# The down projection of a decoder step as Strassen's seven products over the whole sum, with its operands combined on GpSimd during the up projection

## The chip, the cores and the metric

One core of a Trainium2 chip runs the whole step in one launch. The metric is the device time of one execution in microseconds (us). The engines: TensorE (PE; PEld is its weight load), VectorE (DVE), ScalarE (ACT), GpSimd (POOL, "Pool" below) and SyncE (SP), which issues most DMAs.

## The reference

One inference step of a hybrid decoder layer: 1024 prompt tokens and 8 x 8 sample tokens, 1088 rows of 1024 channels. After the mixing sub-layer comes the channel sub-layer, which the change is about:

```python
    h2 = x * (1 + sc2) + sh2
    val, gt = jnp.split(h2 @ w_up, 2, axis=-1)
    gt_c, ffn_state = _causal_dwconv(gt, ffn_prev, w_fdw, b_fdw)
    f = (jax.nn.gelu(gt_c, approximate=False) * val) @ w_down
    x = _layernorm(ALPHA * x + (1 + g2) * f, ln2_g, ln2_b)
```

Here `w_up` is 1024 x 5632, `w_down` 2816 x 1024, the convolution 3 wide, and all values are float32.

## The kernel before, in words

Matmul operands are held in two parts: `split` (L551 to L553) writes a rounded high part on ScalarE (L552, type fp32r) and the residue on VectorE (L553). A product takes three passes for the prompt rows (high x high, high x low, low x high), and two for the sample rows, whose two parts share one stationary tile.

**Up projection.** A column block f (of NFF = 22, 128 channels of the value and 128 of the gate) is one step. It already runs by Strassen's seven products (in Winograd's form) over its block: `up_weights(f)` loads the gate's and the value's weights (L1724, L1725, into the ring `raw` of three buffers), Pool makes four combinations of 512 columns (L1728, L1729, L1730, L1733), and seven splits write the weight tiles W[0] to W[6], each held once, so that W[i] of the next block is written after product i of this block. `up` (matmuls at L1752) walks through the seven products; `evacuate` adds partial results into the tiles `vt` (value) and `gp` (gate) with the operations at L1675 to L1687, each reading PSUM. `gate` applies the width-3 convolution on VectorE (L1769 to L1773, into `gc`), gelu on ScalarE (L1774) and the product with the value on Pool (L1776, 128 x 1088); then SyncE stores the block to the DRAM scratch `fscr` (L1777) and its sample columns to `fsscr` (L1778). Blocks run in the order f = 0, 1, ..., 21.

**Down projection.** The 22 blocks are summed in three groups, GROUPS = (0..7), (8..14), (15..21). In each group all nine row tiles (eight of the prompt, `tt` = 8 for the sample) are multiplied by the group's weights:

```python
    for grp, (f0, f1) in enumerate(GROUPS):
        for tt in range(9) if grp < 2 else (8, *range(8)):
...
            fx, passes = f_tile(grp, tt)
...
            for i in range(nf):
...
                for xt, wt in passes:
                    for c in cs_:
                        PE.matmul(pd[c], fx[:, xt, i], w[:, wt, cw * c:cw * c + cw],
...
```

`f_tile` loads a row tile's operands from `fscr` (L1860) and splits them into `ft`; `prefetch` loads and splits whole weight rows of 1024 columns into `wd`, a ring of NW = 12. Group 0 copies its sums into `acc` (L1898), group 1 adds (L1900) and puts in the gated sum and the residual (Pool at L1904 and L1905, VectorE at L1906 and L1907), and group 2 ends each row tile with `finish`: gate, sum, statistics (L1824 to L1827), the norm (L1836 to L1846) and the store of `y`.

The order of instructions on each engine is set by the framework's scheduler before the run; at run time each engine takes its instructions strictly in that order.

## Time and profile before

| | |
|---|---|
| median of three runs | 1494.72 us (1490.79 to 1496.66) |
| the profiled execution: its own time | 1499.9 us |
| the profiled execution: its span | 1498.1 us, 27014 instructions |
| busy: PE / DVE / ACT / POOL | 1425.9 / 1102.5 / 611.2 / 579.4 us |
| up projection | about 775 to 1221 us of the span |
| down projection | 1226 to 1498 us |
| HBM read / written | 184.31 / 32.68 MB |

The span is what the profile covers; the execution's own time lies 1.8 us over it. Times in the rows further down are counted from the span's start. A duration of VectorE or ScalarE overlaps with the next instruction's by some 0.08 us, so that the step from start to start is a little shorter than the busy time.

### The profile page before, as it was taken

To read this page: it belongs to the slowest core of one execution; us is meant where nothing else is said; L and a number is where in the kernel's file an instruction comes from. 1 tells how busy PE (TensorE), PEld (TensorE's weight loads), DVE (VectorE), ACT (ScalarE), POOL (GpSimd) and SP (SyncE) were. 2 spreads that over 40 slices of the span, in tenths; PEclk is the share of its full clock that TensorE was granted. 3 is DMA by queue.
4 is the path that set the end of the run, shared out by engine and by line. 5 is a ranking of instruction groups with operands and counts; after the bars stand their busy time and mean duration, and the time that the engine had idled before them with its cause. 6 is when DMAs were issued, how large, how long until landed. Compare 5 with 4: busy or idle time off the path is not lost.

```text
span 1498.1 us, 27014 instructions
## 1 busy us (share of the span) xinstructions
PE 1425.9 (95%) x10302; PEld 1237.2 (83%) x10302; DVE 1102.5 (74%) x1935; ACT 611.2 (41%) x1212; POOL 579.4 (39%) x425
## 2 busy tenths in 40 slices
PE   7999889988999999899989999999999989999997
PEld 4898789985656566578779999999999988888886
DVE  5799999447576756767778777778777764268798
ACT  2534414627787868614353333333333333031110
POOL 0497722116353543524344444344433422016300
PEclk9999999989999999999989999999999999999999
DMA  9755432155868777453213222222222257142331
GB/s 340 244 173 173 149 118 96 73 218 184 289 253 294 270 256 282 159 163 119 77 62 101 73 87 72 82 67 85 75 84 73 73 151 263 47 161 87 112 99 70
DMA packets 116987, 219.26 MB, mean 146 GB/s; under 512 B 28673, under 2 KB 71210, under 8 KB 116602
## 3 DMA queue, kind: packets, MB, share of 16 engines
q1 hardware_dynamic: 113498, 206.03, 41.5%
q0 software_dynamic: 3360, 11.51, 2.1%
q8 instruction: 81, 1.33, 0.3%
q14 instruction: 48, 0.39, 0.1%
HBM read 184.31 MB, written 32.68 MB: 145 GB/s over the span
## 4 chain that ended last, share of the span: by engine, by line
PE 65%; DVE 4%; DMA 2%; ACT 2%; issue 1%; POOL 1%; SPq 0%; DVEq 0%; POOLq 0%; ACTq 0%
PE pu L1752 22%; PE pd L1883 18%; PE scr L1752 7%; PE pu L1451 3%; PE z L1062 2%; PE scr L1451 2%; PE acc L1072 2%; PE acc L1261 2%; PE scr L1205 2%; DMA kv<-kv 1%; PE z L1017 1%; PE z L1022 1%; PE scr L1244 1%; ACT l L820 1%; DVE lh L1055 1%
## 5 line engine op out<-in xcount | busy, mean ns | idle before, releaser
L1883 PE MATMUL pd<-wd,ft 128*128 128x512 f32 (+1 forms) x1186 | 263.0, 385 | 4.4 <-ACT ft L552 4.4
L1883 PEld LDWEIGHTS pd<-wd,ft 128*128 128x128 f32 x1186 | 218.7, 190 | 48.7 <-ACT ft L552 5.0
L1752 PE MATMUL pu<-X,wA 128*128 128x272 f32 x768 | 187.6, 288 | 0.0
L1752 PE MATMUL pu<-Y,wA 128*128 128x272 f32 x756 | 186.7, 288 | 0.0
L1058 POOL TENSOR_TENSOR ll<-l,lh 127x512 fp32r<-127x512 f32 (+4 forms) x92 | 98.2, 1070 | 154.2 <-DVE lh L1055 108.9
L589 PE MATMUL po<-HH,whi 128*128 128x378 f32 (+1 forms) x464 | 152.7, 338 | 0.0
L589 PE MATMUL po<-HL,whi 128*128 128x378 f32 (+1 forms) x464 | 151.8, 333 | 0.5 <-DVE HL L553 0.4
L589 PE MATMUL po<-HH,wlo 128*128 128x378 f32 (+1 forms) x464 | 151.6, 333 | 0.0
L820 ACT ACTIVATE l<-z 127x512 f32<-127x512 f32 (+14 forms) x272 | 121.0, 478 | 52.7 <-PE z L1022 19.6
L1752 PEld LDWEIGHTS pu<-X,wA 128*128 128x128 f32 x768 | 141.5, 188 | 0.0
L1752 PEld LDWEIGHTS pu<-Y,wA 128*128 128x128 f32 x756 | 140.7, 189 | 0.0
L677 DVE SCALAR_TENSOR_TENSOR pc<-u,vec,pc 128x1024 f32<-128x1024 f32 x80 | 102.6, 1282 | 1.3
L1728 POOL TENSOR_TENSOR cc__8820<-raw 128x512 f32<-128x512 f32 x20 | 36.6, 1830 | 168.6 <-DMA raw<-w_up 151.4
L589 PEld LDWEIGHTS po<-HH,whi 128*128 128x128 f32 x464 | 87.1, 190 | 7.9 <-ACT whi L552 3.3
L589 PEld LDWEIGHTS po<-HH,wlo 128*128 128x128 f32 x464 | 87.6, 190 | 4.3 <-issue 3.7
L553 DVE TENSOR_TENSOR wA<-raw,wA 128x512 fp32r<-128x512 f32 x60 | 75.8, 1263 | 20.2 <-ACT wA L552 20.1
L589 PEld LDWEIGHTS po<-HL,whi 128*128 128x128 f32 x464 | 86.9, 188 | 3.9 <-issue 1.7
L661 POOL TENSOR_TENSOR cv<-cv,q 128x1024 f32<-128x1024 f32 x36 | 88.7, 2464 | 3.1 <-ACT q L660 1.4
L552 ACT ACTIVATE wA<-raw 128x512 fp32r<-128x512 f32 x60 | 38.0, 633 | 121.8 <-PE pu L1752 65.6
L1027 DVE SCALAR_TENSOR_TENSOR l<-l,z 127x512 f32<-127x512 f32 (+4 forms) x96 | 53.2, 556 | 38.8 <-ACT l L820 37.9
L1055 DVE CAST lh<-l 127x512 fp32r<-127x512 f32 (+4 forms) x96 | 51.7, 542 | 35.9 <-ACT l L820 24.0
L552 ACT ACTIVATE ft<-fr 128x896 fp32r<-128x896 f32 (+3 forms) x27 | 25.5, 943 | 126.4 <-PE pd L1883 121.5
(654 smaller groups left out, 3633.0 us busy)
## 6 DMA issues: line engine op xcount, KB each, us to landing
kv<-kv SPq DMA_DIRECT2D x128, 512.0 KB
catt<-w_ada SPq DMA_DIRECT2D x48, 512.0 KB
...
```

What stands on the lines that cost most here:

```text
L552: A.activation(hi, x, AF.Copy)
L553: V.tensor_sub(lo, x, hi)
L589: PE.matmul(ps[c][:, 0:b - a], wt[:, 128 * kt:128 * kt + 128], xt[:, kt, a:b], start=first and kt == 0, stop=last and kt == KT - 1)
L661: G.tensor_tensor(op, op, t[:, 0:TP], op=OP.add)
L677: V.scalar_tensor_tensor(pcs[c], src, w, pcs[c], op0=OP.mult, op1=OP.add)
L820: A.activation(out, in_, f, **kw)
L1027: V.scalar_tensor_tensor(out, e, ZMAX, z, op0=OP.min, op1=OP.max)
L1055: V.tensor_copy(t.hl[0], t.l)
L1058: (V if eng == "DVE" else G).tensor_tensor(t.hl[1], t.l, t.hl[0], op=OP.subtract)
L1451: PE.matmul(po[c](), xs()[:, xt, kt % 4], WO[kt][:, wt, 512 * c:512 * c + 512], start=kt == KORD[0] and (xt, wt) == passes[0], stop=kt == ...
L1752: PE.matmul(p[g][:, 0:NB], W[i][wt][:, 128 * kt:128 * kt + 128], X[g][kt][xt][:, i, :], start=i < 3 and kt == 0 and n == 0, stop=kt == 3 a ...
L1883: PE.matmul(pd[c], fx[:, xt, i], w[:, wt, cw * c:cw * c + cw], start=i == 0 and (xt, wt) == passes[0], stop=i == nf - 1 and (xt, wt) == pa ...
```

## The change

The order of blocks in the up projection becomes f = 0, 11, 1, 12, ..., 10, 21, so that after every second block the tiles f = j and f = j + 11 are both on the chip. `combine` lets Pool make four combinations of them (128 x 512 each) and SyncE stores these to a DRAM scratch `sscr`. `down_weights` loads a half of the down projection's weight rows j and j + 11, lets Pool make four combinations (128 x 256 each) in the one buffer `tw`, and SyncE stores them to the scratch `tscr`. For a block f < 11 only the first half of its prompt columns is stored to `fscr`. The buffer `gc` of the gate is held once instead of twice.

The down projection then takes the whole sum of 22 blocks as a 2 x 2 problem: rows 0..511 and 512..1023, blocks 0..10 and 11..21, columns 0..511 and 512..1023, with seven products s of 11 tiles each (s = 0 to 5 and 7), operand by operand of the weights; s = 6 holds weights that only the sample rows need, which are multiplied without combining. Weights are loaded in halves of 512 columns (88 loads for 22), the ring `wd` holds NW = 18 of them, and row tiles of 11 x 128 columns are loaded per product. `half` does gate, residual and statistics of a row tile's half as soon as its sum is complete, `finish` the norm.

```diff
-NW = 12
+NW = 18
-GROUPS = ((0, 8), (8, 15), (15, NFF))
+NH = NFF // 2
+FO = [f for j in range(NH) for f in (j, j + NH)]
...
+    sscr = drp.tile([128, 4, NH, 512], F32, "sscr")
+    tscr = drp.tile([NH, 2, 128, D], F32, "tscr")
...
-        c = dp.tile([128, 4, NB], F32, "gc", bufs=2)
+        c = dp.tile([128, 4, NB], F32, "gc", bufs=1)
...
-        SY.dma_start(fscr[:, :, f, :], v4[:, :, 0:256])
+        n = 2 if f < NH else 4
+        SY.dma_start(fscr[:, 0:n, f, :], v4[:, 0:n, 0:256])
...
+    def combine(j, va, vb):
+        (a11, a21), (a12, a22) = ([v[:, h, :, 0:256] for h in range(2)] for v in (va, vb))
+        so = [dp.tile([128, 2, 256], F32, "so", bufs=2) for _ in range(2)]
+        def one(o, x, y, op, k):
+            G.tensor_tensor(o, x, y, op=op)
+            SY.dma_start(sscr[:, k, j, :].rearrange("p (g i) -> p g i", g=2), o)
+        one(so[0], a21, a22, OP.add, 0)
+        one(a21, a11, a21, OP.subtract, 2)
+        one(so[1], so[0], a11, OP.subtract, 1)
+        one(dp.tile([128, 2, 256], F32, "so", bufs=2), a12, so[1], OP.subtract, 3)
...
+    def down_weights(j, c):
+        t = dp.tile([128, 2, 2, 256], F32, "tw", bufs=1)
+        part = lambda a: a.rearrange("p (b x) -> p b x", b=2)[:, :, 256 * c:256 * c + 256]
+        for i in range(2):
+            SY.dma_start(t[:, i], part(d["w_down"][j + NH * i]))
+        b11, b12, b21, b22 = (t[:, i, b] for i in range(2) for b in range(2))
+        G.tensor_tensor(b11, b12, b11, op=OP.subtract)
+        G.tensor_tensor(b12, b22, b12, op=OP.subtract)
+        G.tensor_tensor(b22, b22, b11, op=OP.subtract)
+        G.tensor_tensor(b21, b22, b21, op=OP.subtract)
+        for i in range(2):
+            SY.dma_start(part(tscr[j, i]), t[:, i])
...
-    for f in range(1, NFF):
-        if f > 1:
+    for n in range(1, NFF):
+        f = FO[n]
+        if n > 1:
             up_weights(f)
...
         gelu = gate(f, *t)
+        if n % 2:
+            combine(n // 2, before, v)
+        down_weights((n - 1) // 2, (n - 1) % 2)
+        before = v
+    down_weights(NH - 1, 1)
...
+    def half(tt, c, parts=1):
...
+        x = ep.tile([128, 512], F32, "fx", bufs=2)
+        SY.dma_start(x[0:n], xscr[t0:t0 + n, H[c]])
+        G.tensor_tensor(x[0:n], x[0:n], rows[0][0:n, 0, H[c]], op=OP.mult)
+        G.tensor_tensor(x[0:n], x[0:n], rows[0][0:n, 1, H[c]], op=OP.add)
...
+        def rest(i):
...
+            V.tensor_mul(a[0:n, p], a[0:n, p], g2["p" if tt < 8 else "s"][0:n, H[c]][:, p])
+            V.tensor_add(a[0:n, p], a[0:n, p], x[0:n, p])
+            V.bn_stats(fst[tt][0:n, parts * c + i, :], a[0:n, p])
...
+    SRC_W = [(lambda j, i=i, c=c: d["w_down"][j + NH * i][:, H[c]]) if k == "b" else (lambda j, i=i, c=c: tscr[j, i][:, H[c]])
+             for k, i, c in (("b", 0, 0), ("b", 1, 0), ("t", 1, 0), ("t", 1, 1), ("t", 0, 1), ("t", 0, 0), ("b", 0, 1), ("b", 1, 1))]
+    SRC_A = [plain(0, 0), plain(0, 1), plain(2, 1), mixed_(1), mixed_(2), mixed_(0), None, mixed_(3)]
...
+    def product(p, lhs, s, passes, cs, start=True, stop=True):
+        for j in range(NH):
+            w = ws[NH * s + j]
+            for x, k in passes:
+                PE.matmul(p, lhs(x, j), w[:, k, cs], start=start and j == 0 and (x, k) == passes[0],
+                          stop=stop and j == NH - 1 and (x, k) == passes[-1])
...
+    for s in range(8):
+        if s > 5:
+            prefetch(NH * (s + 1))
+            sample(s)
...
+        for q in range(4):
+            lhs = a_tile(s, q)
+            prefetch(NH * (s + 1))
...
+            product(p, lhs, s, FULL, ALL)
+            if s == 0:
+                A.activation(c22, p, AF.Copy)
+            elif s == 1:
+                V.tensor_add(c11, c22, p)
...
+            elif s == 5:
+                V.tensor_add(c22, c22, p)
+                V.tensor_add(c12, c12, p)
+                half(q + 4, 1)(0)
+                finish(q + 4)
+            else:
+                V.tensor_add(c12, c12, p)
+                half(q, 1)(0)
+                finish(q)
+            prefetch(min(len(ws) + 3, NH * s + NW))
```

What the scheduler makes of it on Pool, in the middle of the up projection. Before, one block's five operations, in this order (`cc__8820` is the buffer of one combination, `raw` the loaded weights, `vt` and `gc` value and gate):

```order
L1728 TENSOR_TENSOR cc__8820<-raw 128x512
L1729 TENSOR_TENSOR raw<-raw 128x512
L1730 TENSOR_TENSOR raw<-cc__8820,raw 128x512
L1776 TENSOR_TENSOR vt<-vt,gc 128x1088
L1733 TENSOR_TENSOR raw<-raw 128x512
```

After, a stretch of the first half of the blocks: the last of one block's sums, the gelu product (now L1780), and up to the next block's first sum (now L1732):

```order
L1733 TENSOR_TENSOR raw<-raw 128x512
L1807 TENSOR_TENSOR tw<-tw 128x256
L1734 TENSOR_TENSOR raw<-cc__8822,raw 128x512
L1780 TENSOR_TENSOR vt<-vt,gc 128x1088
L1808 TENSOR_TENSOR tw<-tw 128x256
L1793 TENSOR_TENSOR so<-vt 128x512
L1809 TENSOR_TENSOR tw<-tw 128x256
L1793 TENSOR_TENSOR vt<-vt 128x2x256
L1793 TENSOR_TENSOR so<-so,vt 128x512
L1810 TENSOR_TENSOR tw<-tw 128x256
L1737 TENSOR_TENSOR raw<-raw 128x512
L1793 TENSOR_TENSOR so<-vt,so 128x512
```

The four sums of one `tw` group (L1807 to L1810) stand between the sums that feed the next block's weights. Behind these rows come L1807, L1808, L1809, L1732 and L1810 of the next group, then L1733, L1734 and L1780; in the following block two groups stand in one piece each. Groups go on so, two to a block, through the first ten blocks of the loop and end there; in the second half a pair of blocks holds its ten operations of before and the four combinations of L1793.

SyncE in the same stretch, after (before, it held `raw`, `raw`, `fscr` and `fsscr` per block and nothing else):

```order
L1812 DMA tscr<-tw 256x1x256
L1794 DMA sscr<-so 128x512
L1794 DMA sscr<-vt 128x2x256
L1794 DMA sscr<-so 128x512
L1812 DMA tscr<-tw 256x1x256
L1805 DMA tw<-w_down 128x2x256
L1794 DMA sscr<-so 128x512
L1805 DMA tw<-w_down 128x2x256
L1729 DMA raw<-w_up 128x1024
L1812 DMA tscr<-tw 256x1x256
L1728 DMA raw<-w_up 128x1024
L1812 DMA tscr<-tw 256x1x256
```

A weight load for the next block (L1728, L1729) stands behind the stores and loads of `tw`, each of which waits for Pool or for the store before it.

VectorE in the down projection, product s = 5, one row tile (`pd` is PSUM, `fr` and `raw` are the loaded operands, now split at L557):

```order
L1991 TENSOR_TENSOR acc_14318<-acc_14318,pd 128x512
L1992 TENSOR_TENSOR acc_14314<-acc_14314,pd 128x512
L1886 SCALAR_TENSOR_TENSOR fw<-fw 128x1
L557 TENSOR_TENSOR ft<-fr,ft 128x1408
L1870 TENSOR_TENSOR acc_14318<-acc_14318,g2p 128x512
L557 TENSOR_TENSOR wd<-raw,wd 128x512
L1887 TENSOR_SCALAR fw<-fw 128x1
L1871 TENSOR_TENSOR acc_14318<-acc_14318,fx 128x512
L1888 TENSOR_TENSOR fw<-fw 128x1
L1872 BN_STATS fs_14327<-acc_14318 128x6
L1890 SCALAR_TENSOR_TENSOR fy<-fy,fw,rows_14806 128x512 x2
L1881 BN_AGGR fw<-fs_14327 128x2
```

The splits for the coming products (L557) stand in one queue with the sums, the gate and the norm of the row tiles that are finished.

## Rows read from the trace of the kernel before

**Rows 1.** the page's first part: busy time, share of the span, instructions.

```profile
PE 1425.9 (95%) x10302; PEld 1237.2 (83%) x10302; DVE 1102.5 (74%) x1935; ACT 611.2 (41%) x1212; POOL 579.4 (39%) x425
```

**Rows 2.** stretches: length, busy us of PE, PEld, DVE, ACT, POOL, clock, DMA share, GB/s.

```profile
1000.00:1100.00 100.00, 100.00 (x801) 100.00 (x800) 77.05 (x148) 31.66 (x67) 39.91 (x24) 1.00 0.26 80
...
1300.00:1350.00 50.00, 50.00 (x223) 41.40 (x222) 27.79 (x27) 12.35 (x13) 5.86 (x2) 1.00 0.41 131
...
1400.00:1450.00 50.00, 50.00 (x223) 41.40 (x222) 44.88 (x67) 8.52 (x16) 5.04 (x2) 1.00 0.35 108
```

**Rows 3.** single lines and the tile raw: duration ns min/median/max, first and last start us.

```profile
L1733 POOL TENSOR_TENSOR raw<-raw x20: 1285/1291/1630, 796.6 to 1192.8; 128x512 f32<-128x512 f32 x20
...
L1776 POOL TENSOR_TENSOR vt<-vt,gc x22: 2527/2535/4138, 791.8 to 1228.8; 128x1088 f32<-128x1088 f32 x22
...
L553 DVE TENSOR_TENSOR wd<-raw,wd x22: 1211/1224/2960, 1223.4 to 1407.6; 128x1024 fp32r<-128x1024 f32 x22
```

**Rows 4.** Pool in time: start us, us, engine, line, operation, idle before.

```profile
950.16 1.31 POOL L1728 TENSOR_TENSOR cc__8820<-raw 128x512 f32<-128x512 f32 x1 [8.42 <-DMA raw<-w_up]
951.54 2.16 POOL L1729 TENSOR_TENSOR raw<-raw 128x512 f32<-128x512 f32 x1
954.53 1.30 POOL L1730 TENSOR_TENSOR raw<-cc__8820,raw 128x512 f32<-128x512 f32 x1 [0.83 <-DVE wA L553]
955.80 2.54 POOL L1776 TENSOR_TENSOR vt<-vt,gc 128x1088 f32<-128x1088 f32 x1
```

**Rows 5.** VectorE in time, the same columns.

```profile
950.24 2.31 DVE L1772 SCALAR_TENSOR_TENSOR gc<-gp,vec,gc 128x1024 f32<-128x1024 f32 x1
...
954.31 0.41 DVE L1677 TENSOR_TENSOR gp<-vt,pu 128x256 f32<-128x256 f32 x1
...
956.54 2.35 DVE L553 TENSOR_TENSOR wA<-raw,wA 128x512 fp32r<-128x512 f32 x1 [0.66 <-ACT wA L552]
...
966.89 0.68 DVE L553 TENSOR_TENSOR cb__8914<-raw,cb__8914 128x512 fp32r<-128x512 f32 x1
967.49 0.17 DVE L1760 COPY fop<-gp 128x2 f32<-128x2 f32 x1
967.56 0.81 DVE L1769 TENSOR_SCALAR gc<-gp,vec 128x1024 f32<-128x1024 f32 x1
...
968.58 1.28 DVE L1772 SCALAR_TENSOR_TENSOR gc<-gp,vec,gc 128x1024 f32<-128x1024 f32 x1
969.78 0.28 DVE L1773 SCALAR_TENSOR_TENSOR gc<-gs,vec,gc 128x64 f32<-128x64 f32 x1
...
1422.44 1.22 DVE L1831 TENSOR_TENSOR acc<-acc,fx 64x1024 f32<-64x1024 f32 x1 [4.49 <-DMA fx<-acc]
```

**Rows 6.** SyncE in time, the same columns.

```profile
946.57 0.33 SPq L1725 DMA_DIRECT2D raw<-w_up  x1
...
1417.98 0.51 SPq L1830 DMA_DIRECT2D fx<-acc  x1
```

**Rows 7.** waits, 800 to 1200 us: who waited, total us, times, longest.

```profile
POOL cc__8820 L1728 <- DMA raw<-w_up: 140.2, 17, 8.6
```

**Rows 8.** operations by form, 1225 to 1500 us: busy us, mean ns, idle before.

```profile
L1883 PE MATMUL pd<-wd,ft 128*128 128x512 f32 x1102 | 253.0, 392 | 4.4 <-ACT ft L552 4.4
...
L1846 DVE SCALAR_TENSOR_TENSOR fy<-fy,fw,rows 128x512 f32<-128x512 f32 x16 | 11.3, 748 | 0.2
...
L1839 DVE SCALAR_TENSOR_TENSOR fy<-acc,fw,rows 128x1024 f32<-128x1024 f32 x8 | 10.3, 1283 | 0.2
L1883 PE MATMUL pd<-wd,ft 128*128 128x256 f32 x84 | 10.2, 283 | 0.0
```

**Rows 9.** stretches at the start of the down projection, columns as in rows 2.

```profile
1226.00:1235.00 9.00, 9.00 (x27) 6.76 (x28) 8.49 (x7) 6.41 (x6) 4.14 (x1) 0.67 0.93 284
```

**Rows 10.** TensorE in time, columns as in rows 4.

```profile
1225.94 6.30 PE L1883 MATMUL pd<-wd,ft 128*128 128x512 f32 x14 [4.37 <-ACT ft L552]
```

**Rows 11.** the chain that ended last, 1470 to 1498 us.

```profile
1469.83 19.15 PE pd L1883 x124
```

More of the change, by code (lines that the diff above doesn't have):

```diff
@@ L1800, in body, with load_rows @@
     acc = [ep.tile([128, D], F32, f"acc{i}") for i in range(9)]
-    rows, g2 = [None, None], {}
-    def load_rows(i):
-        rows[i] = ep.tile([128, 2, D], F32, "rows", bufs=1)
-        SY.dma_start(rows[i], d["lnr"][2 * i:2 * i + 2].unsqueeze(0).to_broadcast([128, 2, D]))
-        if i == 0:
-            A.activation(rows[0], rows[0], AF.Copy, scale=ALPHA)
+    fst = [ep.tile([128, 4, 6], F32, f"fs{i}") for i in range(9)]
+    rows, g2 = [], {}
+    H = [slice(0, 512), slice(512, 1024)]
+    def load_rows():
+        for i in range(2):
+            rows.append(ep.tile([128, 2, D], F32, f"rows{i}"))
+            SY.dma_start(rows[i], d["lnr"][2 * i:2 * i + 2].unsqueeze(0).to_broadcast([128, 2, D]))
+        A.activation(rows[0], rows[0], AF.Copy, scale=ALPHA)
     def load_gates():
@@ L1843, in finish @@
         V.tensor_tensor(r, q, r, op=OP.mult)
-        for c in range(2):
-            h = slice(512 * c, 512 * c + 512)
+        for h in H:
             V.scalar_tensor_tensor(y[0:n, h], y[0:n, h], r, rows[1][0:n, 1, h], op0=OP.mult, op1=OP.add)
             SY.dma_start(d["y"][t0:t0 + n, h], y[0:n, h])
+    SRC_W = [(lambda j, i=i, c=c: d["w_down"][j + NH * i][:, H[c]]) if k == "b" else (lambda j, i=i, c=c: tscr[j, i][:, H[c]])
+             for k, i, c in (("b", 0, 0), ("b", 1, 0), ("t", 1, 0), ("t", 1, 1), ("t", 0, 1), ("t", 0, 0), ("b", 0, 1), ("b", 1, 1))]
@@ new lines, in prefetch, with a_tile @@
+        for k in range(len(ws), min(n, NH * len(SRC_W))):
+            r = raw([128, 512])
+            SY.dma_start(r, SRC_W[k // NH](k % NH))
+            w = wdp.tile([128, 2, 512], F32R, "wd", bufs=NW)
+            split(r, w[:, 0], w[:, 1])
+            ws.append(w)
+    def a_tile(s, q):
+        fr = wdp.tile([128, NH, 128], F32, "fr", bufs=2)
+        fx = wdp.tile([128, 2, NH, 128], F32R, "ft", bufs=2)
+        SY.dma_start(fr, SRC_A[s](q))
+        split(fr, fx[:, 0], fx[:, 1])
+        return lambda x, j: fx[:, x, j]
@@ new lines, in body, with sample, sample_finish @@
+    FULL, PAIR = ((0, 0), (0, 1), (1, 0)), ((0, 0), (0, 1))
+    ALL = slice(0, 512)
+    sums = [psE.tile([128, 512], F32, f"ps{i}") for i in range(2)]
+    def sample(s):
+        k, c = (0, 1, None, None, None, None, 0, 1)[s], s // 6
+        product(sums[c], s_tile(k), s, PAIR, ALL, start=k == 0, stop=k == 1)
+        if k:
+            V.tensor_copy(acc[8][:, H[c]], sums[c])
+    def sample_finish():
+        x = ep.tile([128, D], F32, "fy", bufs=2)
+        SY.dma_start(x[0:TS], acc[8][TS:128])
+        V.tensor_add(acc[8][0:TS], acc[8][0:TS], x[0:TS])
+        for c in range(2):
+            half(8, c)(0)
+        finish(8)
@@ new lines, in body @@
+    for s in range(8):
+        if s > 5:
+            prefetch(NH * (s + 1))
+            sample(s)
+        if s == 6:
+            continue
+        if s == 7:
+            sample_finish()
+        for q in range(4):
+            lhs = a_tile(s, q)
+            prefetch(NH * (s + 1))
+            last = (s, q) == (7, 3)
+            (c11, c12), (c21, c22) = ([acc[t][:, h] for h in H] for t in (q, q + 4))
+            if last:
+                rest = half(q, 1, 2)
+                for i in range(2):
+                    p = psE.tile([128, 512], F32, "pd", bufs=6)[:, 0:256]
+                    cs = slice(256 * i, 256 * i + 256)
+                    product(p, lhs, s, FULL, cs)
+                    V.tensor_add(c12[:, cs], c12[:, cs], p)
+                    rest(i)
+                finish(q, 2)
+                continue
+            p = psE.tile([128, 512], F32, "pd", bufs=6)
+            product(p, lhs, s, FULL, ALL)
[3 more added lines that the diff above has]
+                V.tensor_add(c11, c22, p)
+            elif s == 2:
+                A.activation(c21, p, AF.Copy, scale=-1.0)
+            elif s == 3:
+                V.tensor_add(c12, c22, p)
+                parts = 2 if q == 3 else 1
+                rest = half(q, 0, parts)
+                for i in range(parts):
+                    rest(i)
+            elif s == 4:
+                V.tensor_add(c22, c12, p)
+                V.tensor_add(c21, c21, c22)
+                half(q + 4, 0)(0)
+            elif s == 5:
[8 more added lines that the diff above has]
+            prefetch(min(len(ws) + 3, NH * s + NW))
+            if (s, q) == (0, 2):
+                load_gates()
+            if (s, q) == (1, 2):
+                load_rows()
+        if s < 2:
+            sample(s)
```

97 lines of the change are left out of this document (22 added, 75 removed).

## Prediction

> **What bounds the kernel now.** The page's first part comes first: TensorE is busy 95% of the span, VectorE 74%, GpSimd (Pool) 39% [rows 1]. That is an average, so the second view is the table by stretches. In the up projection (1000 to 1100 us) TensorE is busy all the time at full clock, 801 matmuls in 100 us [rows 2]. One column block f takes 7 products x 4 row tiles x 3 passes x 2 halves = 168 matmuls, 168 / 8.01 = 20.97 us, and two blocks 41.9 us. VectorE works 77 us of the 100 there, Pool 40. In the down projection TensorE is busy throughout too, 223 matmuls in 50 us, 0.224 us each, while VectorE climbs from 28 to 45 of 50 us [rows 2]. So both stages wait for TensorE alone: fewer matmuls pay in full, and anything that holds TensorE up costs in full.
>
> The third view is the order of VectorE and Pool side by side. Pool's sum of 512 takes 1.29 us and its gelu product of 1088 takes 2.54 when alone [rows 3]. At 955.80 the product starts; VectorE's residue of a weight, 0.68 us elsewhere, begins at 956.54 and takes 2.35, to just after the product's end [rows 4, 5]. At 950.24 a multiply-add of 1.28 waits out a Pool sum and takes 2.31; the next Pool sum then waits for it (2.16 for 1.29). But the evacuation at 954.31, one operand in PSUM, runs in 0.41 beside Pool's sum of 954.53 [rows 4, 5]. So Pool and those VectorE operations that read two SBUF operands take turns, whole instruction by whole instruction. For these the two engines are one resource, and its load is the sum of both.
>
> **The matmuls that go.** Before: 1102 of 512 columns and 84 of 256 [rows 8]. After, by count of the code: seven products x 4 row pairs x 11 tiles x 3 passes, the last in halves, and 88 for the sample rows: 979 and 66. 123 x 0.224 = 27.6 us and 18 x 0.121 (10.2 us / 84, rows 8) = 2.2: **-29.8 us**, in full if TensorE stays fed.
>
> **Pool during the up projection.** The diff suggests some six more small operations per block. The order of instructions says more: the weight combinations, 22 groups of four sums of 256 columns, aren't spread over the 21 blocks. Two groups stand ahead of the loop, and the other 20 stand two to a block in the first ten, in between the sums that make the next block's weights. So five pairs of blocks carry all of it.
>
> Price of a sum of 256: from 1.29 (512) and 2.54 (1088) the slope is 2.16 ns a column, so 0.74 us. One pair of blocks then has on Pool: 8 x 1.29 + 2 x 2.54 = 15.4 (as now), four activation combinations 4 x 1.29 = 5.2, sixteen weight sums 11.8: 32.4 us. VectorE's two-operand work per block is seven residues, which follow each other 0.60 apart (966.89 to 967.49), two multiply-adds 1.20 apart (968.58 to 969.78) and two small ones of 0.20 [rows 5]: 7.0 us, 14.0 a pair. Together 46.4 us of a resource that has 41.9: the **floor**, 4.5 us a pair over. Whether the large tensor-scalar (0.81 busy at 967.56) takes turns as well, these rows don't tell: it ran with Pool idle. The Trainium skill (SBUF — State Buffer, Who interferes with whom) says that a tensor_scalar with one SBUF input can enter a mode that uses both ports and then takes turns too; by that, at 0.72 from start to start, the floor would be 47.8.
>
> Second limit, the chain of one buffer. `tw` has a single buffer: four sums, store, load, next four sums, and Pool's queue is strictly in the written order, so a group that waits for its load stops everything behind it. By the order rows the four groups of a pair hold, from first to last sum, the group's own 4 x 0.74 plus what stands between: 1.29 + 2.54 + 3 x 1.29 in one, 1.29 in another, nothing in two: 10.7 + 4.3 + 3.0 + 3.0 = 20.9 us. Between groups come a store and a load. A 512 KB load issued at 946.57 releases Pool at 950.16, 3.6 us; a 256 KB copy issued at 1417.98 releases VectorE at 1422.44, 4.5 us [rows 4 to 6]. At 3.6 each, four gaps of 7.2 make 49.7 us a pair; at 4.5, 56.9. Collisions with VectorE inside the groups come on top. What Pool has to do in the gaps (1.3 to 5.1 us) fits into them, so it adds nothing. The Trainium skill (DMA: Bandwidth & Descriptors, Anatomy of one DMA — SWDGE (gpsimd) path) gives 2.0 us plus bytes over 436 GB/s; by that estimate a gap would be 5.8 and the chain 44, under the floor. The row for the load (3.6 against 3.2 by that fit) is above it, so I stay with the rows.
>
> I take 51 us a pair, near the chain at 3.6 with a little collision; ends 46.4 and 56.9. Over five pairs that is 5 x 9.1 = 45 us of lag. Part of it is absorbed. The gelu product ends at 958.34 and the next block's first gate operation, which now shares the one buffer `gc` with it, comes at 967.56: 9.2 us of slack [rows 4, 5]. The second weight's residue ends at 958.89, and its matmuls start one block after those that ended near 954.3, less a product of 3 us: 13 us. The waits show the same looseness: in 400 us of this stage Pool now idles 140 us for loads of `w_up` [rows 7]. I take 10 us off: **+35 us** (ends 12 and 65). In the second ten blocks only 5.2 us a pair is added, 20.6 + 14.0 = 34.6 of 41.9: nothing. `fscr` writes less, the combined operands go out by SyncE beside a DMA share of 0.26 [rows 2]: nothing, unless a store held up in SyncE's queue holds a weight load behind it, and that wait ends with Pool's lag, already counted.
>
> **The down projection's own new costs.** Start: the first product wants 11 half-weights (256 KB) and two operand tiles (720 KB), 4.2 MB, in the 7.4 us of its first 33 matmuls. At the same place the kernel now moves 284 GB/s at a DMA share of 0.93, and does 27 matmuls in 9 us where 40 fit [rows 9]: 15 us for these bytes, against 7.4. That is 7.6 more; now 2.9 (13 matmuls) are lost there already, and loads can start a little ahead: **+6** (0 to 10).
>
> End: VectorE. From the sixth product (s = 5) on: ten operand residues (eight of 1408 columns, 1.55 each by 0.68 for 512 and 1.22 for 1024 [rows 3, 5]) 14.0; 22 weight residues x 0.60 = 13.2; 13 additions or copies out of PSUM 7.8; ten halves' gate, residual and statistics 18.0; one sample addition 1.2; nine final norms, 1.20 + 2 x 0.66 [rows 8], less the 0.08 by which neighbours overlap, and six small ones, 3.3 each, 29.7: 84 us. TensorE needs there 275 x 0.224 + 66 x 0.121 = 69.8, plus the tail of today, 9.1 (the last matmul ends at 1489.0 [rows 11] of a span of 1498.1). VectorE ends 3 us before the end: 87 against 79, +8. Pool's 20 residual sums of 1.29 fall in the same stretch; if half collide, 13 more. **+14** (5 to 24). Earlier products leave VectorE room (s = 4: 25 of 29.6 us).
>
> **Sum.** -29.8 + 35 + 6 + 14 = +25. The profiled execution took 1499.9 us (span 1498.1): 1525. It lies 5.2 over the median of the runs (1494.72), so on that scale **1520 us**. By the ends of the up projection's term alone the forecast's own range is 1497 to 1550.
>
> **Rivals.**
> *The lag never reaches TensorE.* It decides at the point where a pair's lag times five stays under the slack: 2.2 to 2.6 us a pair, that is a store and load in under 5.8 us together and collisions that fall in VectorE's idle time. For it: Pool is idle 60% now, TensorE never waits in this stage. Against: the floor of 46.4. Then only the down projection counts, and with VectorE keeping up (+5) and no start cost it gives -25, with both -10: 1470 to 1485, say **1477**. Chance 0.18. It is the side on which the kernel is faster, and only here.
> *A draw.* The floor holds without more: 5 x 4.5 - 10 = +12, against -10 in the down projection: **1497** (1488 to 1502). Chance 0.12. By the fit for a DMA named above it would end here.
> *The stalls also cost clock.* TensorE's pause of 4.4 us before 1225.94 [rows 10] is followed by 9 us at a mean granted clock of 0.67 of 2.4 GHz [rows 9], part of them at 1.2 GHz: 3 us lost. If each of ten stalled blocks pauses that long in one piece, 30 us more: **1550**. Against: the waits are spread over seven products. The Trainium skill (TensorE: Matmul & The Clock Gate, What's actually happening) says the throttled state is the default and activity releases it; whether short waits do it, no row here shows. Chance 0.10.
> That fewer matmuls aren't issued is excluded by the count in the code.
>
> **Numbers.** Forecast 0.60. Half a per cent (7.5 us) is about what a measurement of this kernel can tell from no change. The forecast and the clock rival are slower: 0.70; the draw 0.11 with its edges; faster 0.19. Two in ten left out puts the range at 1477 to 1553.
>
> **What would show it.** Right: in the new profile, five pairs of blocks from about 800 us each take about 51 us, TensorE's busy share there falls to 0.8, the waits show Pool's sums waiting for `tw` loads, ScalarE or VectorE for Pool's weight sums, and TensorE for evacuations; the later ten blocks take 21 us each again; the down projection is some 10 us shorter, with TensorE waiting in s = 6 and 7. Wrong: blocks of 21 us throughout (then the taking of turns or the store and load are cheaper than I read), or a down projection shorter by 25 (then VectorE at the end is not a bound).

## The result, and the profile after

The changed kernel takes **1562.6 us** (median of four runs, 1560.2 to 1563.8) against 1493.2 for the kernel before on the same chip: a ratio of 1.046, 95% interval 1.043 to 1.048. The direction was forecast, the size was not: 1520 was said, with a range up to 1553.

The profiled span grew from 1498.1 to 1560.2 us, by 62.1. Two places hold all of it. "Behind" is from the last matmul of the up projection to the end of the span.

| us | before | after | difference | predicted |
|---|---|---|---|---|
| up projection ends | 1221.6 | 1264.6 | +43.0 | +35 |
| behind | 276.5 | 295.6 | +19.1 | -29.8 + 20 = -9.8 |

The stretches of the changed kernel (columns as in [rows 2]): most of the slow part of the up projection and a stretch of its second half; then, of the down projection, s = 0, s = 1, s = 2 to 4, s = 5, s = 6 and 7, and the tail after the last matmul.

```profile
780.00:1020.00 240.00, 209.62 (x1570) 206.17 (x1568) 156.91 (x287) 63.69 (x137) 170.28 (x137) 0.95 0.50 159
1040.00:1200.00 160.00, 158.32 (x1251) 157.94 (x1250) 130.69 (x230) 51.07 (x107) 98.12 (x60) 0.99 0.34 106
...
1270.30:1311.20 40.90, 36.76 (x133) 27.60 (x134) 20.42 (x20) 18.04 (x25) 9.64 (x5) 0.86 0.87 275
1316.30:1349.30 33.00, 30.70 (x134) 24.46 (x133) 25.05 (x27) 10.05 (x13) 11.31 (x8) 1.00 0.73 218
1354.20:1449.00 94.80, 92.66 (x406) 75.79 (x406) 60.69 (x71) 37.14 (x49) 10.12 (x6) 1.00 0.66 201
1449.00:1481.80 32.80, 30.55 (x125) 23.83 (x123) 32.57 (x43) 12.07 (x20) 15.35 (x8) 0.95 0.57 176
1481.80:1541.10 59.30, 47.86 (x209) 35.74 (x209) 54.45 (x81) 15.76 (x27) 18.96 (x13) 0.91 0.52 160
1541.10:1560.20 19.10, 0.00 (x0) 0.00 (x0) 15.49 (x37) 0.99 (x4) 1.66 (x1) 0.60 0.30 110
```

**Up projection.** At the rate of [rows 2], 801 matmuls in 100 us, the 240 us of the first row hold 1922; there were 1570. The 352 that are missing are worth 43.9 us, as much as the whole lag. 30.4 us of them TensorE stands idle; the other 13.6 come from matmuls that are slower, 209.62 / 1570 = 0.1335 us each instead of 0.1248, at a mean granted clock of 0.95. In the second row the rate is almost that of before. From one gelu to the gelu two blocks later it takes 48.5, 52.9, 51.7 and 53.3 us in the middle of the first half, and 40.0 to 42.1 later.

**Behind.** 132 matmuls of 512 columns take 29.6 us at 0.224 each. s = 0 takes 40.9 and s = 1 33.0; s = 2 to 4, with 94.8 for 88.7, and s = 5 lose less. In s = 5 VectorE is busy 32.57 of 32.80 us, in s = 6 and 7 54.45 of 59.30, and then for another 15.49 after the last matmul.

What is waited for between 780 and 1020 us (columns as in [rows 7]):

```profile
ACT wA L556 <- POOL raw L1734: 67.1, 10, 9.9
DVE wA L557 <- ACT wA L556: 65.6, 12, 9.6
POOL tw L1807 <- DMA tw<-w_down: 38.0, 15, 4.8
ACT cb__8916 L556 <- POOL raw L1737: 37.8, 7, 8.4
...
POOL cc__8822 L1732 <- DMA raw<-w_up: 21.4, 6, 5.4
```

Pool's third and fourth sum of a block's weights (L1734, L1737) come late, and Pool itself waits for two kinds of loads. Pool in time (columns as in [rows 4]) shows both:

```profile
898.39 1.32 POOL L1807 TENSOR_TENSOR tw<-tw 128x256 f32<-128x256 f32 x1 [4.46 <-DMA tw<-w_down]
899.79 1.59 POOL L1808 TENSOR_TENSOR tw<-tw 128x256 f32<-128x256 f32 x1
901.46 1.21 POOL L1809 TENSOR_TENSOR tw<-tw 128x256 f32<-128x256 f32 x1
902.75 0.73 POOL L1810 TENSOR_TENSOR tw<-tw 128x256 f32<-128x256 f32 x1
906.06 1.27 POOL L1732 TENSOR_TENSOR cc__8822<-raw 128x512 f32<-128x512 f32 x1 [2.57 <-DMA raw<-w_up]
```

At 898.39 the second `tw` group has waited 4.46 us for its load; its sums take 1.2 to 1.6 us where 0.73 is what one takes alone; and the next block's first sum then waits for a load of `w_up`.

Operations from 1264 us on (columns as in [rows 8]):

```profile
L1928 PE MATMUL pd<-wd,ft 128*128 128x512 f32 x891 | 218.7, 403 | 19.0 <-ACT ft L556 11.9 <-DVE ft L557 6.9 <-ACT wd L556 0.3
...
L556 ACT ACTIVATE wd<-raw 128x512 fp32r<-128x512 f32 x88 | 53.5, 628 | 88.0 <-DMA raw<-tscr 42.7 <-DMA raw<-w_down 39.3 <-PE pu L1756 3.7
...
L1864 POOL TENSOR_TENSOR fx<-fx,rows 128x512 f32<-128x512 f32 x16 | 26.5, 1657 | 184.1 <-DMA fx<-xscr 166.5 <-DVE acc L1870 17.5
L1928 PE MATMUL ps<-wd,ft 128*128 128x512 f32 x88 | 25.5, 419 | 8.9 <-DVE wd L557 7.0 <-ACT wd L556 1.4 <-DVE ft L557 0.4
...
L1870 DVE TENSOR_TENSOR acc<-acc,g2p 128x512 f32<-128x512 f32 x14 | 13.9, 995 | 0.1
...
L1928 PE MATMUL pd<-wd,ft 128*128 128x256 f32 x66 | 8.1, 283 | 0.0
```

The matmuls are those forecast: 891 + 88 = 979 of 512 columns and 66 of 256. Of what stands here the sum had none or too little: ScalarE waits 82 us for loads of weights; VectorE's gate (L1870) takes 995 ns and Pool's residual sum (L1864) 1657, where each is shorter alone (686 ns for the gate in r8 below, 1.29 us for a sum of this size on Pool [rows 3]).

### The profile page after: what moved, and what is told of

It reads as the page before. It is cut to its first block, busy times and chain, and to the rows that moved or that the text cites. A ratio compares the mean times of both kernels' runs of the same rounds, so it can differ in the third digit from the quotient of the medians.

```text
span 1560.2 us, 27533 instructions
## 1 busy us (share of the span) xinstructions
PE 1423.6 (91%) x10161; PEld 1224.5 (78%) x10161; DVE 1153.6 (74%) x1983; ACT 656.0 (42%) x1291; POOL 730.7 (47%) x575
## 4 chain that ended last, share of the span: by engine, by line
PE 30%; DMA 12%; DVE 9%; POOL 8%; issue 5%; ACT 2%; SPq 1%; DVEq 0%; POOLq 0%; ACTq 0%
PE pu L1756 11%; PE pd L1928 5%; DMA tw<-w_down 4%; PE scr L1756 3%; DMA tscr<-tw 3%; PE pu L1455 3%; DMA raw<-w_down 2%; PE scr L1455 2%; POOL tw L1808 2%; DMA raw<-tscr 2%; DVE wd L557 1%; POOL tw L1809 1%; POOL tw L1810 1%; DVE acc L1870 1%; PE acc L1076 1%
## 5 line engine op out<-in xcount | busy, mean ns | idle before, releaser
L1928 PE MATMUL pd<-wd,ft 128*128 128x512 f32 (+1 forms) x957 | 226.7, 395 | 19.0 <-ACT ft L556 11.9
L1928 PEld LDWEIGHTS pd<-wd,ft 128*128 128x128 f32 x957 | 179.5, 194 | 64.0 <-ACT ft L556 15.3
L557 DVE TENSOR_TENSOR wA<-raw,wA 128x512 fp32r<-128x512 f32 x60 | 84.4, 1407 | 74.7 <-ACT wA L556 74.5
L1864 POOL TENSOR_TENSOR fx<-fx,rows 128x512 f32<-128x512 f32 (+1 forms) x18 | 29.0, 1614 | 196.4 <-DMA fx<-xscr 178.8
L557 DVE TENSOR_TENSOR wd<-raw,wd 128x512 fp32r<-128x512 f32 x88 | 70.2, 829 | 30.0 <-ACT wd L556 29.9
L556 ACT ACTIVATE wd<-raw 128x512 fp32r<-128x512 f32 x88 | 53.5, 628 | 88.0 <-DMA raw<-tscr 42.7
L1031 DVE SCALAR_TENSOR_TENSOR l<-l,z 127x512 f32<-127x512 f32 (+4 forms) x96 | 53.1, 555 | 37.7 <-ACT l L824 36.8
```

What stands on the lines that cost most here:

```text
L556: A.activation(hi, x, AF.Copy)
L557: V.tensor_sub(lo, x, hi)
L1031: V.scalar_tensor_tensor(out, e, ZMAX, z, op0=OP.min, op1=OP.max)
L1928: PE.matmul(p, lhs(x, j), w[:, k, cs], start=start and j == 0 and (x, k) == passes[0], stop=stop and j == NH - 1 and (x, k) == passes[-1])
```

## The experiments

The up projection and what lies behind it can be read apart in one run, so from the fifth run on a kernel holds an edit in each. r2, r3, r5, r7, r8 and r10 leave out a part of the work; they show what that part costs and are not complete kernels. All results in one table (us; "up end" and the stretches are of the profiled execution; s = 2 to 5 from its first matmul to its last, s = 6, 7 from there to the last matmul of all, in r4 s = 7 alone; ratio to the kernel before on the same chip):

| run | median | ratio, 95% | up end | behind | s=0 | s=2-5 | s=6,7 | tail |
|---|---|---|---|---|---|---|---|---|
| before | 1493.2 | | 1221.6 | 276.5 | | | | 9.1 |
| after | 1562.6 | 1.043-1.048 | 1264.6 | 295.6 | 40.9 | 127.3 | 59.6 | 19.1 |
| r1_spread | 1535.2 | 1.025-1.030 | 1229.0 | 304.5 | 39.8 | 128.1 | 59.2 | 20.0 |
| r2_nosum | 1546.4 | 1.032-1.037 | 1247.9 | 297.9 | 40.0 | 128.6 | 56.9 | 21.0 |
| r3_nodma | 1535.7 | 1.026-1.030 | 1238.5 | 295.1 | 41.6 | 128.0 | 56.9 | 20.6 |
| r4_s6early | 1570.2 | 1.049-1.053 | 1266.3 | 301.1 | 41.4 | 133.4 | 47.3 | 23.7 |
| r5_pin_nosum | 1520.5 | 1.014-1.022 | 1245.0 | 275.1 | 42.7 | 120.6 | 51.1 | 13.7 |
| r6_bal_ring | 1534.7 | 1.023-1.030 | 1251.8 | 283.1 | 35.5 | 120.1 | 55.8 | 20.5 |
| r7_bal_nofin | 1557.5 | 1.037-1.048 | 1249.7 | 301.3 | 46.2 | 128.8 | 52.1 | 20.6 |
| r8_floor | 1483.5 | 0.991-0.996 | 1220.0 | 260.0 | 34.9 | 119.9 | 45.0 | 14.5 |
| r9_best | 1505.1 | 1.007-1.010 | 1220.1 | 280.8 | 34.3 | 123.5 | 57.7 | 13.6 |
| r10_aq | 1538.4 | 1.026-1.034 | 1271.6 | 270.6 | 35.1 | 120.3 | 47.0 | 21.2 |
| r11_resid | 1500.1 | 1.002-1.005 | 1221.5 | 279.0 | 34.8 | 137.9 | 46.9 | 12.7 |
| r12_residq | 1497.3 | 1.000-1.004 | 1224.6 | 279.0 | 34.7 | 129.9 | 47.3 | 13.2 |

### The up projection: amount, store and load, or SyncE's order

**r1_spread**: each group of weight sums is held, on Pool, behind its own block's gelu product, one group to a block.

```diff
+        gm[0] = G.tensor_tensor(v4, v4, c, op=OP.mult).ins
...
+        with tc.issue_after(gm[0]):
+            down_weights((n - 1) // 2, (n - 1) % 2)
```

> The changed kernel with the weight sums spread: each of the 22 groups is ordered on Pool behind the gelu product of its own block, so one group stands in each block instead of two in each of the first ten. Amount of work unchanged. In the changed kernel pairs of the first ten blocks took 48.5 to 53.3 us instead of 41.9, and the up projection ended at 1264.6 instead of 1221.6 us. Chain theory (store and load of the one buffer stand in Pool's written order): a pair then holds two gaps of 7 us and its work, which fit into 41.9: the up projection ends at 1222 to 1230, the total falls by 35 to 43 to 1520 to 1527. Turns theory (Pool and VectorE's two-operand work share one resource): 26.5 + 14.0 = 40.5 us of 41.9 a pair fits just, 1520 to 1535. Rival (each group costs TensorE 2 us wherever it stands): the end stays near 1264, total above 1550.

The lag falls from 43 to 7.4 us, with every sum, store and load still there: it was the crowding, two groups to a block. A pair of blocks takes 43.4 us. The total misses the 1520 to 1527 of the first reading all the same: the stretch behind is 8.9 us longer than in the changed kernel, 7.3 of it from the first matmul of s = 0 to the first of s = 2 (91.2 for 83.9). The last groups' loads and stores now stand in SyncE's queue among the first loads of the down projection; with six loads under way (r8) that stretch is 75.1.

**r2_nosum**: the four weight sums are left out.

```diff
-        G.tensor_tensor(b11, b12, b11, op=OP.subtract)
...
-        G.tensor_tensor(b21, b22, b21, op=OP.subtract)
```

> The changed kernel without the four Pool sums of the weight groups (the down projection's combined weights are left out: the raw weights are stored in their place); the loads and stores of the buffer stay. Chain theory and turns theory alike: Pool waits for no such load, the up projection ends at 1222 plus or minus 4, total 1517 to 1524. Rival (SyncE's queue or the added DMA traffic holds the next block's weight loads up): the end stays over 1240, total over 1538.

This is the rival's range, but it doesn't decide: with nothing on Pool to hold them, the transfers moved forward into the first seven blocks, up to four groups to a block, and these take up to 29 us each. It does show a lag of 26 us in which Pool has no weight sum of the down projection.

**r3_nodma**: the reverse. The sums stay two groups to a block (with r1's `issue_after`, for n < 12); their loads and stores go, and the down projection takes uncombined weights.

```diff
-        for i in range(2):
-            SY.dma_start(part(tscr[j, i]), t[:, i])
```

> The changed kernel with the 22 groups of weight sums, pinned two to a block for the first eleven blocks, but without their loads and stores: all groups work on one buffer that is loaded once, and the down projection takes the uncombined weights (so the weight combination is left out of the result). Pool's work and its collisions with VectorE stay, store and load in Pool's order are gone. Chain theory: pairs of the first blocks take 42 to 44 us, the up projection ends at 1222 to 1230, total 1518 to 1528. Turns theory: pairs take 46.4 to 48, five of them, the end is at 1235 to 1250, total 1532 to 1546.

The gelu of three blocks in a row:

```profile
895.05 1.12 ACT L1778 ACTIVATE gc<-gc 128x1088 f32<-128x1088 f32 x1 [4.14 <-DVE gc L1777]
919.50 1.11 ACT L1778 ACTIVATE gc<-gc 128x1088 f32<-128x1088 f32 x1 [7.56 <-DVE gc L1777]
940.93 1.11 ACT L1778 ACTIVATE gc<-gc 128x1088 f32<-128x1088 f32 x1 [5.50 <-DVE gc L1777]
```

24.5 + 21.4 us make 45.9, and most pairs take 45.8. That is close to the floor of turns that the prediction worked out, 46.4. So the sums alone cost 3.9 us a pair, and a lag of 17.

**r5_pin_nosum**, up: no sums, and the transfers meant to be held two groups to a block. Down: the residual's gain and bias on Pool are left out.

```diff
+            with tc.issue_after(gm[0]):
+                for c in range(2):
+                    down_weights(n - 1, c)
...
-        G.tensor_tensor(x[0:n], x[0:n], rows[0][0:n, 0, H[c]], op=OP.mult)
-        G.tensor_tensor(x[0:n], x[0:n], rows[0][0:n, 1, H[c]], op=OP.add)
```

> Two edits, read apart at the end of the up projection. Up: the weights' sums on Pool are left out (so tscr holds uncombined weights), their loads and stores stay, two groups to a block in the first eleven blocks. If the wait for store and load in Pool's order is what cost the other half of the lag, nothing on Pool waits any more and the up projection ends at 1221 to 1227. If SyncE's queue holds the w_up loads back behind these transfers, it ends after 1236. Down: the residual's two Pool instructions in half (gain and bias) are left out, the plain row is added. If Pool's collisions with VectorE bound the end, the stretch from the end of the up projection to the end of the span falls from 295.6 to 276 to 283 us; if VectorE's own amount of work bounds it, it stays at 290 to 297.

The hold didn't take: as in r2 the transfers moved forward, up to four groups to a block, and ended with the eighth block, so r5 repeats r2 here and doesn't show what SyncE's order costs at two groups to a block. What it shows is a lag of 23 us though Pool has nothing of `tw` to wait for. SyncE's queue in time, and Pool's first sum:

```profile
875.61 1.25 SPq L1805 DMA_DIRECT2D tw<-w_down  x2
878.50 0.56 SPq L1808 DMA_DIRECT2D tscr<-tw  x1
879.16 0.55 SPq L1729 DMA_DIRECT2D raw<-w_up  x1
879.76 0.57 SPq L1808 DMA_DIRECT2D tscr<-tw  x1
880.43 0.55 SPq L1728 DMA_DIRECT2D raw<-w_up  x1
```

```profile
870.65 1.29 POOL L1793 TENSOR_TENSOR so<-vt,so 128x512 f32<-128x512 f32 x1
883.79 1.29 POOL L1732 TENSOR_TENSOR cc__8822<-raw 128x512 f32<-128x512 f32 x1 [11.84 <-DMA raw<-w_up]
```

The load that Pool waits 11.84 us for goes out at 880.43, behind a load and two stores of `tw`, each of which waits for the one before it. The down part of this run comes below.

**r10_aq**, up: the changed kernel with the `w_up` loads on ScalarE's queue. Down: r6's loads, and the norm of row tiles 4 to 7 left out.

```diff
-        SY.dma_start(rg, d["w_up"][NFF + f])
+        A.dma_start(rg, d["w_up"][NFF + f])
...
-                finish(q + 4)
```

> Up: the changed kernel with only the loads of w_up moved to ScalarE's queue; the sums stay two groups to a block. If SyncE's order is all that the lag has beyond the 17 us of Pool's turns, it ends at 1236 to 1244; if Pool's own wait for the second group's store and load counts as well, at 1250 to 1262. Down: the loads of r6, and the norm of row tiles 4 to 7 left out. If VectorE's amount bounds s=6 and 7 once the loads are cured, that stretch falls from r6's 56 us to 44 to 50 and the whole behind the up projection to 266 to 273; if not, 52 to 56 and 275 to 280.

Up: 1271.6, above both readings; its other execution was 11.7 us shorter, so that the 7 us over the changed kernel tell nothing, but no gain shows. Pool's own waits say why (780 to 1020 us):

```profile
POOL tw L1807 <- DMA tw<-w_down: 61.1, 16, 7.9
POOL cc__8822 L1732 <- DMA raw<-w_up: 8.3, 2, 5.3
```

The wait for `w_up` is all but gone, that for `tw` has grown by 23 us, and pairs take 52 to 55. With two groups to a block Pool's wait for the one buffer holds the block up whatever queue `w_up` is on. What SyncE's order costs can be read at one group to a block: with `w_up` on ScalarE's queue as well (r8 below, which in the up projection differs from r1 in that alone) the up projection ends at 1220.0 instead of r1's 1229.0, in pairs of 24.1 + 18.3 us. That the lag beyond the 17 us of turns is the chain of the one buffer is argued from the waits and from r1; a second buffer for `tw`, which would test it directly, was not run.

### Behind: s = 0 to 7

**r4_s6early**: s = 6 between s = 1 and 2, so that VectorE's queue holds no weights for the sample rows at the end.

```diff
-    for s in range(8):
+    for s in (0, 1, 6, 2, 3, 4, 5, 7):
```

> The changed kernel with the sample rows' own set of weights (s = 6) taken third instead of next to last, between s = 1 and s = 2; everything else unchanged. In the changed kernel TensorE lost 19 us in s = 6 and 7 (59 us for 40 us of matmuls), and 19 us passed from its last matmul to the end, against 9 before. Theory VectorE-bound (from s = 5 on VectorE has more work than TensorE): only the 11 residues and one operand that move away come off, 8 to 10 us: total 1552 to 1555. Theory weights-bound (at s = 6 and 7 the 15 weights that the ring could not hold come in too late): the 19 us go, total 1541 to 1546. Rival (the loss moves to the new place, as 11 more weights are wanted in 5 us there): total 1560 to 1565.

The total, 1570.2, lies above all three readings; nearest is the rival, that the loss moves. Behind s = 5 the matmuls end 12.3 us sooner, of which 4.9 are the 22 sample matmuls that moved away, but the tail is 4.6 longer, the way from the first matmul of s = 0 to the first of s = 2 7.3 and s = 2 to 5 6.2: the stretch behind grew by 5.5 us.

**r5_pin_nosum**, down: 275.1, just under the range that the theory of collisions gave. s = 6, 7 falls by 8, the tail by 5.4. s = 2 to 5 falls by 6.7 too. In the changed kernel one line of it, L1864, holds 26.5 us of Pool's time, the other 28.9, and VectorE has to take turns with them.

**r6_bal_ring**, up: two groups in every second block. Down: two half-width loads share a slot of `raw`, six under way instead of three.

```diff
+            if k % 2 == 0:
+                rr[0] = raw([128, 2, 512])
+            r = rr[0][:, k % 2]
-            r = raw([128, 512])
```

> Two edits, read apart at the end of the up projection. Up: the groups of weight sums go to the blocks that hold no combine (two in each even block, one in block 1, three in block 20). If Pool's amount per block against VectorE's two-operand instructions sets the lag, it ends at 1222 to 1230; if each second group of a block costs a store and a load in Pool's order wherever it stands, at 1236 to 1245. Down: two half-width weight loads share one slot of raw, so six can be under way instead of three. If the three-slot ring holds the loads back in s=0 to 5, the stretch from the end of the up projection to the end of the span falls from 295.6 to 271 to 281 us; if the DMA engines are full or VectorE is, it stays at 289 to 297. Total by the favourable readings 1493 to 1511, by the others 1525 to 1542.

Down: from the first matmul to the last 251.4 us instead of 270.8: 5.4 less in s = 0, 2.7 in s = 1, 7 in s = 2 to 5, 3.8 in s = 6 and 7. The stretch as defined fell only to 283.1, since its first matmul came 11.2 us after the up projection (5.7 before), behind a third group in the last even block. What ScalarE waits for, from 1263 us on:

```profile
ACT wd L556 <- DMA raw<-w_down: 20.4, 14, 6.9
...
ACT wd L556 <- DMA raw<-tscr: 13.2, 5, 4.3
```

34 us of waits instead of 82. The loads were late for want of slots, not because the DMA engines were full: in s = 0 r9, with six under way, moves 324 GB/s where the changed kernel moved 275. The rate alone doesn't tell whether loads are late: r7, with three, moves 286 and r10, with six, 268. Up: 1251.8, above both readings and worse than one to a block: blocks alternate between 18 to 19.5 and 25 to 30 us. So the second group of a block costs wherever it stands; that the price is a store and a load is argued.

**r7_bal_nofin**: up as r6; down, the norm and stores of row tiles 4 to 7 left out.

```diff
                 half(q + 4, 1)(0)
-                finish(q + 4)
```

> Up: as r6, the same expectation for its end. Down: the norm and the stores of row tiles 4 to 7 after s=5 are left out. If VectorE's amount of work from s=5 on bounds the end, its some 13 to 16 us leave the stretch: 279 to 284 us after the end of the up projection; if the loads or Pool's late residual sums bound it, 290 to 297.

301.3: the expectation is missed. s = 6, 7 gives 7 us, but the first matmul comes 12.3 us after the up projection (5.7 before), as in r6, and the loads, three at a time, lose 5 more in s = 0 (46.2). With the loads cured (r10) the same edit gives s = 6, 7 in 47.0 and 270.6 in all, as expected there. Both rows of s = 6 and 7 with the norm, r6, and without, r10:

```profile
1458.60:1514.40 55.80, 47.48 (x210) 36.50 (x209) 55.39 (x83) 14.79 (x25) 19.47 (x10) 0.91 0.53 161
```

```profile
1473.90:1521.00 47.10, 41.69 (x210) 34.37 (x208) 41.64 (x53) 13.20 (x19) 17.00 (x10) 1.00 0.47 140
```

In r6 VectorE is busy 55.39 of 55.80 us: here it is the bound. The same 210 matmuls take 47.48 us at a granted clock of 0.91 and 41.69 at 1.00, so 6 of the 9 us come back as clock; TensorE's pauses fall only from 8.3 to 5.4 us.

### Both together, and what is left

**r8_floor**: r1's order, `w_up` on ScalarE's queue, six loads under way, and the residual's gain and bias left out (the edits of r1, r10, r6 and r5).

```diff
+        A.dma_start(rg, d["w_up"][NFF + f])
...
+            r = rr[0][:, k % 2]
...
-        G.tensor_tensor(x[0:n], x[0:n], rows[0][0:n, 0, H[c]], op=OP.mult)
```

> Up: one group of weight sums per block behind the gelu product (as r1_spread), and the loads of w_up are issued from ScalarE's queue, so nothing of the down weights stands ahead of them. If SyncE's order makes up the 7 us that r1_spread kept, the up projection ends at 1221 to 1226; if Pool's amount does, at 1227 to 1231. Down: two half-width loads to a slot of raw (as r6) and the residual's gain and bias left out (as r5). If loads and collisions are separate losses, the stretch behind the up projection is 259 to 268 us; if both edits cure the same loss, 272 to 278. Total 1480 to 1494 or 1499 to 1509.

1483.5, the low end of it. The lag is gone, and loads and collisions add up: 295.6 becomes 277.6 by the loads (r6's 283.1 with its start put at 5.7) and 260.0 without Pool's residual sums. Of these 17.6 us 10.8 stand in s = 6 and 7 and 6.0 in the tail. s = 2 to 5 lose nothing by the sums once the loads are cured: r6 takes 120.1 us with them,

```profile
1338.50:1458.60 120.10, 120.10 (x529) 98.87 (x528) 89.21 (x111) 48.38 (x68) 30.79 (x15) 1.00 0.67 207
```

and r8 119.9 without. The 7 us that they lose in the changed kernel end by either cure (r5, r6).

**r9_best**: the same with the residual in place, and four `fx` tiles.

```diff
-        x = ep.tile([128, 512], F32, "fx", bufs=2)
+        x = ep.tile([128, 512], F32, "fx", bufs=4)
```

> Up as r8_floor, same expectation (1221 to 1226 against 1227 to 1231). Down: the loads of r6, the residual in place, with four fx tiles instead of two. If the residual's late loads are what pushes Pool's sums into the last stretch, the stretch behind the up projection is 268 to 275 us; if Pool's and VectorE's amounts are, 276 to 281. Total 1489 to 1501 or 1497 to 1512; before is 1494.

The second reading: 280.8, and 1505. Four `fx` tiles did not cure it. The two kernels at s = 2 to 5 and s = 6, 7, r8 first:

```profile
1300.60:1420.30 119.70, 119.70 (x529) 99.13 (x528) 83.67 (x116) 48.69 (x68) 0.00 (x0) 1.00 0.68 213
1420.30:1465.50 45.20, 42.23 (x210) 34.32 (x208) 44.38 (x82) 14.73 (x25) 0.00 (x0) 1.00 0.62 193
```

```profile
1306.00:1431.80 125.80, 120.61 (x531) 98.86 (x529) 95.23 (x114) 49.36 (x69) 26.50 (x16) 1.00 0.62 195
1431.80:1487.30 55.50, 48.08 (x209) 37.98 (x209) 55.36 (x91) 13.69 (x24) 17.91 (x8) 0.88 0.53 166
```

Beside Pool's 26.5 and 17.9 us of busy time VectorE's is 11.6 and 11.0 longer. TensorE's stretches are 3.6 and 12.7 longer by the table; these rows are cut at the first sample matmul, which in r9 comes 2.2 us after the last of s = 5. r9 also loses 5.3 us before s = 2 (80.4 for 75.1), and ScalarE waits there and in s = 2 for weight loads, so the two kernels' difference isn't Pool's collisions alone.

**r11_resid** works the residual of ten halves out early, in s = 2 and 3, and stores it back; **r12_residq** does the early loads and stores on Pool's queue.

```diff
+        G.tensor_tensor(x[0:n], x[0:n], rows[0][0:n, 0, H[c]], op=OP.mult)
+        G.tensor_tensor(x[0:n], x[0:n], rows[0][0:n, 1, H[c]], op=OP.add)
+        SY.dma_start(xscr[t0:t0 + n, H[c]], x[0:n])
```

> r9_best with the residual (gain and bias on Pool) of the ten halves that s=5 to 7 need worked out in s=2 and 3 and stored back to xscr, so that later only loads are left of it. Nothing is left out. If Pool's collisions with VectorE in the last 100 us are the 21 us by which r9_best stands above r8_floor, and s=2 to 4 have room for them (DMA share 0.57 to 0.75, VectorE two thirds busy there), the stretch behind the up projection is 260 to 268 us and the total 1482 to 1490, under before's 1494. If the collisions only cost the same elsewhere, or the extra 5 MB of transfers hold the weights up, it stays at 274 to 282 and 1497 to 1507.

> r11_resid with the early residual's loads and stores on Pool's own DMA queue instead of SyncE's. r11_resid gave back in s=2 and 3 (136 us for s=2 to 5 instead of 120) what it won behind them. If SyncE's order (stores that wait for Pool, weights' loads behind them) is that loss, s=2 to 5 return to 120 to 125 us, the stretch behind the up projection to 262 to 268 and the total to 1483 to 1491. If it is the extra transfers themselves or Pool's collisions with VectorE, the stretch stays at 273 to 282 and the total at 1495 to 1506.

In both the end becomes as short as r8's (s = 6, 7 in 47, tail 13), and s = 1 to 3 lose it again: in r11 s = 2 to 5 takes 138 us and s = 1 31.4, in r12 130 and 38.5. What r12 wins in the one it loses in the other, and both stand at 279.0 behind the up projection: that SyncE's order is part of the loss isn't shown. r12 stands at 1.002 (1.000 to 1.004): no better than before. r11's rows for s = 2, s = 3, and s = 4 and 5:

```profile
1303.00:1340.40 37.40, 32.48 (x134) 25.96 (x133) 21.14 (x19) 13.66 (x19) 26.16 (x16) 0.91 0.88 273
1340.30:1381.10 40.80, 33.97 (x134) 26.50 (x133) 31.42 (x31) 11.70 (x15) 17.29 (x13) 0.92 0.63 188
1381.10:1440.70 59.60, 59.60 (x264) 49.38 (x263) 51.57 (x77) 22.93 (x34) 0.00 (x0) 1.00 0.67 208
```

VectorE and Pool together are busy 47.3 us in 37.4 and 48.7 in 40.8; in s = 4 and 5, 51.6 in 59.6, some room was left. One of the stalls in time, VectorE and then TensorE:

```profile
1342.38 10.67 DVE L557 TENSOR_TENSOR wd<-raw,wd 128x512 fp32r<-128x512 f32 x4
```

```profile
1350.82 1.47 PE L1944 MATMUL pd<-wd,ft 128*128 128x512 f32 x3 [4.05 <-DVE wd L557]
```

Four residues of weights, 0.67 us each elsewhere, take 10.67, while Pool works eight residual sums off one behind the other, and TensorE waits 4.05 us for one of them. But ScalarE also waits 21.5 us for weight loads in s = 2 and 3, so the loss has two causes and their shares are open. A version that spreads the sums one by one, also over s = 4, wasn't tried. No complete kernel of this design beat the kernel before.

## Why the prediction was wrong

**The matmuls** (-29.8): as forecast, in number (979 and 66) and in worth: where loads and VectorE keep up (r8, s = 2 to 5) 528 matmuls take 119.9 us for 118.3.

**The lag of the up projection** (+35, ends 12 and 65): +43, right in mechanism. The floor of turns, 46.4 us a pair, was measured as 45.8 (r3). The Trainium skill (SBUF — State Buffer, Who interferes with whom) has a VectorE instruction with two SBUF inputs contend with a Pool instruction that reads SBUF; r3 bears it out, with 45.8 us a pair. The chain, 49.7 to 56.9, of which 51 was taken, came out at 48.5 to 53.3 in the changed kernel, 51.6 on average, and 52 to 55 in r10. So the price of a pair was right, and the 10 us taken off for slack were too many. By the Trainium skill's estimate (DMA: Bandwidth & Descriptors, Anatomy of one DMA — SWDGE (gpsimd) path) the chain would have been 44 and the result the draw at 1497; the trace speaks against it with its 51.6, and the rows of before gave the better price. One sentence of the step was wrong in its reason: that the wait for a store held up in SyncE's queue ends with Pool's lag. In r1 Pool's crowding is gone and 7.4 us of lag are left, and they go when `w_up` leaves SyncE's queue (r8).

**The clock.** The rival took 30 us for it in the worst case and gave it 0.10. Some 13.6 us of the lag are slower matmuls (0.1335 for 0.1248 us at a mean clock of 0.95), in the forecast's mechanism: partly right, and in no term of the sum. The down projection has as much again: s = 0 is busy 36.8 us at a clock of 0.86 for 29.8 us of matmuls, and s = 6 and 7 47.9 at 0.91 where r10 needs 41.7 at 1.00. That makes some 27 us, near the 30, but in both stages; it is no sum of its own on top of the others, since part of it falls where TensorE would have waited.

**The down projection's own costs** are the step that failed: "+6" for the start and "+14" for the end, +20 together. Measured are 19.1 + 29.8 = 48.9. By the runs, in the order in which r6 and r8 take them away: 18.0 are weight loads that find no slot, 17.6 Pool's residual sums in VectorE's way, and 13.3 remain in r8, close in sum to the 6 and the 8 that the prediction gave for the first product's loads and for VectorE's amount. Taken the other way round, the sums are worth 20.5 with the loads uncured (r5), so some 3 us belong to both.

- *The loads* were priced for the first product only, as bytes over the rate of [rows 9]. After that they were taken as keeping up. But the change halves each load (256 KB for 512) and keeps three slots, so half as many bytes are under way; in r6 s = 0, 1, 2, 5 and the pair 6 and 7 got shorter by the cure, and ScalarE's waits for weights fell from 82 to 34 us. The sentence "Earlier products leave VectorE room" looked at VectorE alone.
- *The collisions* were bounded by 13 us in s = 5 to 7 ("if half collide") and only 6 of that entered the sum. They cost 17.6, all but 1 of it in s = 6 and 7 and the tail, and part of that as TensorE's clock: 0.91 in r6, 1.00 in r8. A small slip beside it: TensorE's need from s = 5 on adds up to 69.6 us and not 69.8, which moves nothing.

**Rivals.** "The lag never reaches TensorE" and "a draw" needed a lag under 12; both fall with +43. Their other half, a down projection shorter by 10 or 25, falls too: it is 19.1 longer.
